# A hybrid decoder step on one core: tables, raw weight pieces and gathers in other buffers and queues

## The chip, the core and the metric

The kernel runs on one core of a Trainium2 chip. The engines have in-order instruction queues of their own and meet through semaphores: TensorE (PE; its weight loads are listed as PEld), VectorE (DVE), ScalarE (ACT), GpSimd (POOL) and SyncE (SP). SP computes nothing; it issues DMAs. DMAs can be issued by ACT and POOL too; the issue is then an instruction in that engine's queue. The metric is the device time of one execution, in microseconds (us). The kernel before takes 752.33 us, the median of three runs (750.71 to 752.95).

## The reference

One layer on a prompt of 1024 tokens and on 8 single new tokens (samples), each with 256 earlier tokens in paged caches:

```python
hn = rms_norm(x, norm_g)                              # D_MODEL = 1024
u, v, z_a, q, kc, vc, ks, vs, kw, vw, g, z_b = split(hn @ w_in)
# gMLP half: layer norm of v, then a causal 128x128 gate per channel group and chunk
vn = layer_norm(v, ln_v_g, ln_v_b)
a  = u * (einsum('gts,bnsgc->bntgc', w_s * tril, vn) + b_s) * silu(z_a)
# attention half: rope on q, ks, kw; 8 query heads, 2 KV heads, three branches
#   compressed blocks, the 16 selected blocks, a window of 512; gated sum
o  = gate0*attn(q, compress(kc, vc)) + gate1*attn(q, selected(ks, vs)) + gate2*attn(q, window(kw, vw))
y  = rms_norm(x + concat([a, o * silu(z_b)]) @ w_out, final_g)
# samples: the same with pages = cache[page_table]; also returned:
# kc, vc, ks, vs of all tokens, the window's kw, vw, and vn of the samples
```

All data are 32-bit floats. The kernel keeps that accuracy by splitting each operand of a product into a high and a low part (`hi` = a rounded copy, `lo` = the rest) and adding three products: hi·hi, lo·hi and hi·lo.

## The kernel before

*x stage* (lines 192 to 242). Eight pieces of x, each with a piece of w_in for the first three feature groups, are loaded into `raw`. ACT writes the high part `xh` (line 205) and a square, DVE the low part `xl`; PE multiplies piece after piece into tiles `pf` (8 pieces, 24 products of 344 columns each). Lines 244 to 270 make 1/rms: PE sums the squares, DVE spreads the result (`rsb`), and PE transposes it (`pr`) into the row `RS`, by which u and z (`uz`) are scaled on DVE and POOL; `ud` stores a copy of `uz`.

*Queries* (lines 318 to 336). Four tiles of query features, t = 0 to 3, 72 products each (8 pieces x 9), evacuated by ACT and rotated (`rotate`, line 298) with the tables `Cq` and `Sq` of lines 289 and 290; the result goes to `qd` in 4 stores per tile.

*v, k columns, v columns* (lines 349 to 553). Three groups of token tiles, i = 0 to 8 (128 tokens each; tile 8 holds the samples): `ptv` (512 columns), `pta` (384) and `ptb` (408). Tiles 0 to 7 take 24 products and tile 8 takes 16. Each of the first eight `ptv` tiles goes on to ACT (`vt`), DVE (statistics, normalising), POOL (times `lng`, plus `lnb`), ACT again (`vh`, line 450), DVE (`vl`, line 451), and then to 12 products of the gate with the split table `wsh`, `wsl` (`pg`, function `gate`). After a gate, `gather` (line 340) issues two page gathers on SP for one of 16 pages (`cg`, `kg`, DRAM to DRAM, 256 rows of 512 bytes each), and `split_wo` (line 417) loads two 128x512 pieces of w_out (`wost`), splits them on ACT and POOL and stores both parts to DRAM. The `pta` tiles are rotated with `ctok` and `stok` (lines 483, 484), split and transposed on PE (`pkt`, line 524); from here `gather` stands behind each store of k rows. After the `ptb` tiles come compression, attention of the samples, attention of the prompt in query blocks, and the output projection, before which both parts of w_out (`woh`, `wol`) are loaded back.

*Weights.* `load_w` (line 134) loads a raw piece (`wst`, 2 or 3 buffers in the pool that also holds the parts), ACT makes its high part (line 143), DVE its low part (line 144), 9 buffers each. `f_weights` makes two pieces for a feature group, `t_weights` eight for a group of token tiles.

*Order.* A scheduler lays out each engine's instructions by priority and by an estimated timeline, from the program as it is traced; buffers come from pools, and a tile in memory that another pool held waits until that pool's tiles are released. `issue_after(ins)` puts what is issued inside it behind `ins` in its engine's queue. All loads and stores shown here are on SP but the page table's.

## Time and profile before

| | |
|---|---|
| median of three runs | 752.33 us |
| profiled execution, its own time | 751.49 us |
| its span | 749.7 us |
| PE busy | 92% of the span |
| DVE, ACT, POOL busy | 69%, 50%, 39% |
| mean granted clock of PE | 0.97 of full speed |
| moved by DMA | 95.48 MB, of which SP's queue 92.26 |

Times in the rows below count from the span's start. A row of the stretches has its start and end, its length, then for PE, PEld, DVE, ACT and POOL the busy us with the count of instructions, the granted clock, the share of the DMA engines and GB/s. A row of waits has who waited, at which tile and line, for whose tile or transfer, then the total in us, how many times, and the longest. A row of a timeline has start and duration in us, engine and line, tile written and read, shape and count, and in brackets the idle time before it with what ended it. A row of groups has a shape, a count, the busy us, the mean in ns of one and the idle time before. A row of a line's instructions has minimum, median and maximum in ns.

### The profile page before, as it was taken

The page shows a single profiled execution, that of the slowest core. Times are in us where ns is not written, and L with a number is a line of the kernel's source. Part 1 is how long each engine was busy: PE and PEld are TensorE (multiplying, and loading weights), DVE is VectorE, ACT ScalarE, POOL GpSimd, SP SyncE. Part 2 cuts the span into 40 slices and gives each one's busy share as a digit, 9 for nine tenths or more (in the row PEclk, how much of TensorE's full clock was granted, in tenths as well). Part 3 has the DMA queues.
Part 4 walks back from the last instruction along what each step waited for, and adds up shares of the span by engine and source line. Part 5 has one row for each costly group of instructions (what it writes and reads, how often), then busy time and mean ns, then how long its engine had stood idle before and what let it go on. Part 6 is the DMA issues. An engine that isn't in the chain of part 4 may idle for free.

```text
span 749.7 us, 12604 instructions
## 1 busy us (share of the span) xinstructions
PE 688.4 (92%) x4186; PEld 631.7 (84%) x4186; DVE 514.1 (69%) x1470; ACT 374.6 (50%) x890; POOL 293.8 (39%) x282
## 2 busy tenths in 40 slices
PE   8989998778866899999999999998999999999994
PEld 6989986658865799987989999887999998888993
DVE  6737882768724317854279997997777899879743
ACT  7523221233114336431158777886666686666631
POOL 0011434745711003343232244468465656555521
PEclk9999999789988999999999999999999999999997
DMA  8056266657543415427253211895121212212011
GB/s 322 21 197 198 70 155 200 184 190 254 188 138 111 152 29 187 156 81 269 75 162 100 63 62 48 317 315 154 41 70 71 72 43 63 67 59 84 15 57 56
DMA packets 71176, 95.48 MB, mean 127 GB/s; under 512 B 5904, under 2 KB 45440, under 8 KB 70312
## 3 DMA queue, kind: packets, MB, share of 16 engines
q1 hardware_dynamic: 70664, 92.26, 38.6%
q0 software_dynamic: 160, 2.15, 0.8%
q8 instruction: 33, 0.54, 0.3%
q14 instruction: 31, 0.25, 0.1%
q10 hardware_dynamic: 288, 0.27, 0.1%
HBM read 67.85 MB, written 33.10 MB: 135 GB/s over the span
## 4 chain that ended last, share of the span: by engine, by line
PE 53%; DVE 14%; DMA 13%; issue 6%; SPq 5%; ACT 4%; POOL 4%; POOLq 0%; ACTq 0%; DVEq 0%
PE pf L45 15%; PE pout L45 10%; PE o L45 7%; PE S L45 6%; PE pt L940 6%; PE ptb L45 3%; DMA wost<-in_w_out 3%; DMA out<-ka 2%; PE pc L45 2%; DMA wst<-in_wF 1%; DMA wst<-in_w_c 1%; DVE Xl L660 1%; DVE Pl L859 1%; PE po L45 1%; DMA qd<-sh 1%
## 5 line engine op out<-in xcount | busy, mean ns | idle before, releaser
L944 DVE TENSOR_TENSOR tl<-pt,th 128x512 fp32r<-128x512 f32 (+1 forms) x160 | 100.9, 643 | 21.1 <-ACT th L943 20.3
L45 PE MATMUL pf<-xh,whi 128*128 128x344 f32 x384 | 109.4, 326 | 2.1 <-ACT xh L205 1.2
L45 PE MATMUL pf<-xl,whi 128*128 128x344 f32 x384 | 109.9, 322 | 0.0
L45 PE MATMUL pf<-xh,wlo 128*128 128x344 f32 x384 | 109.8, 323 | 0.0
L943 ACT CAST th<-pt 128x512 fp32r<-128x512 f32 (+1 forms) x160 | 83.5, 551 | 27.8 <-PE pt L940 25.9
L917 POOL TENSOR_TENSOR Pw<-Pw,r 128x640 f32<-128x640 f32 (+3 forms) x112 | 76.1, 699 | 52.5 <-DVE r L911 28.0
L45 PE MATMUL pout<-woh,mix 128*128 128x512 f32 (+1 forms) x272 | 87.5, 389 | 1.9 <-ACT mix L977 1.8
L917 POOL TENSOR_TENSOR Pl<-Pl,r 128x384 f32<-128x384 f32 (+5 forms) x36 | 49.3, 1369 | 76.7 <-DVE r L911 30.0
L45 PE MATMUL o<-th,v 128*128 128x256 f32 x264 | 74.3, 300 | 1.4 <-ACT th L943 1.3
L45 PEld LDWEIGHTS pf<-xh,whi 128*128 128x128 f32 x384 | 69.7, 189 | 3.7 <-ACT xh L205 2.1
L45 PEld LDWEIGHTS pf<-xl,whi 128*128 128x128 f32 x384 | 70.3, 190 | 1.0 <-issue 0.6
L45 PEld LDWEIGHTS pf<-xh,wlo 128*128 128x128 f32 x384 | 69.9, 189 | 0.3 <-issue 0.2
L45 PE MATMUL o<-tl,v 128*128 128x256 f32 x264 | 69.7, 289 | 0.4 <-DVE tl L944 0.3
L863 ACT ACTIVATE Pl<-Pl,nmx 128x128 f32<-128x128 f32 (+7 forms) x64 | 49.8, 778 | 23.9 <-DVE nmx L859 18.8
L45 PEld LDWEIGHTS pout<-woh,mix 128*128 128x128 f32 x272 | 50.8, 192 | 11.5 <-ACT mix L977 2.0
L903 ACT ACTIVATE Pw<-Pw,nmx 128x640 f32<-128x640 f32 (+4 forms) x64 | 44.6, 696 | 22.2 <-DVE nmx L895 20.9
L45 PE MATMUL S<-kwS,q 128*128 128x384 f32 (+2 forms) x224 | 52.8, 331 | 1.5 <-DVE nmx L901 0.8
L45 PE MATMUL S<-ksS,q 128*128 128x384 f32 (+5 forms) x192 | 51.8, 357 | 2.4 <-DMA q<-qd 1.9
L45 PEld LDWEIGHTS o<-th,v 128*128 128x128 f32 x264 | 49.9, 189 | 4.4 <-ACT th L943 2.1
L45 PEld LDWEIGHTS o<-tl,v 128*128 128x128 f32 x264 | 49.9, 189 | 4.0 <-DVE tl L944 2.8
L45 PE MATMUL pout<-wol,mix 128*128 128x512 f32 (+1 forms) x136 | 52.5, 387 | 0.0
L144 POOL TENSOR_TENSOR wlo<-wst,whi 128x512 fp32r<-128x512 f32 x18 | 24.1, 1342 | 70.0 <-ACT whi L143 51.5
(337 smaller groups left out, 1698.8 us busy)
## 6 DMA issues: line engine op xcount, KB each, us to landing
q<-qd SPq DMA_DIRECT2D x32, 256.0 KB
wst<-in_wF SPq DMA_DIRECT2D x26, 256.0 KB
raw<-in_xw SPq DMA_DIRECT2D x7, 708.0 KB
wost<-in_w_out SPq DMA_DIRECT2D x16, 256.0 KB
wod<-wohi SPq DMA_DIRECT2D x16, 256.0 KB
wod<-wolo SPq DMA_DIRECT2D x16, 256.0 KB
woh<-wod SPq DMA_DIRECT2D x2, 2048.0 KB
wol<-wod SPq DMA_DIRECT2D x2, 2048.0 KB
```

The costliest lines, as they stand in the source:

```text
L45: return pe.matmul(out, lhsT, rhs, start=start, stop=stop, skip_group_check=True)
L144: e.tensor_tensor(lo[:, :n], st[:, :n], f32(hi[:, :n]), op=ALU.subtract)
L660: v.tensor_tensor(dst(Xl), src, f32(hi), op=ALU.subtract)
L859: v.tensor_tensor_reduce(Pl[:, sl], S[:, 0:half], m, -0.125, nmx[:, 0:1] if c else BIG, ALU.add, ALU.min, nmx[:, 0:1])
L863: s.activation(Pl[:, 0:L], Pl[:, 0:L], AF.Exp, bias=nmx[:, 0:1], scale=-1.0, accum_out=sums[:, 1:2])
L903: s.activation(Pw[:, 0:nw], Pw[:, 0:nw], AF.Exp, bias=nmx[:, 1:2], scale=-1.0, accum_out=sums[:, 2:3])
L917: g.tensor_tensor(t_[:, a:b], t_[:, a:b], r[:, j:j + 1].to_broadcast((P, b - a)), op=ALU.mult)
L940: pe.transpose(pt[:, ci * 256 + e * P:ci * 256 + (e + 1) * P], src[e][:, col:col + P], ident)
L943: s.copy(th[:, :n], pt[:, :n])
L944: v.tensor_tensor(tl[:, :n], pt[:, :n], f32(th[:, :n]), op=ALU.subtract)
```

## The change

- The tables `lng`, `lnb`, `wsh` and `wsl` get a pool of their own (`vq`), loaded between pieces 5 and 6 of x and behind the query weights; `ctok` and `stok` are loaded behind the last query rows.
- Raw pieces get a pool of their own: 4 buffers in the query stage, 8 (`wr`) for the `wTa` and `wTb` pieces; they are issued behind a named DMA (`W["behind"]`): the last x piece, `Sq`, the last query store, the second store of k rows.
- Weights of the first two query tiles are loaded in the x stage, those of the last two behind `Sq`; half of the first query tile's products stand ahead of the transposes of `rsb`.
- The 16 page numbers are loaded into ACT's registers, and ACT issues the gathers. A new function `early` is called behind each `vh`, `k2` and `v2` (24 calls): the first 16 issue one `cg` gather and load and split one 128x512 piece of w_out, the last 8 issue two `kg` gathers each. The store of a low part is issued one call later, by ACT.
- High parts of w_out are no longer stored. Before the output projection w_out itself is loaded again, in 8 pieces of 128x1024, and ACT makes `woh` from them.

The diff, cut to its core:

```diff
-            st = wp.tile([P, 512], F32, tag="wst", bufs=W["raw"], name="wst")
-            with tc.issue_after(x_in.ins):
+            st = W["rp"].tile([P, 512], F32, tag="wst", bufs=W["raw"], name="wst")
+            with tc.issue_after(W["behind"].ins):
                 W["dma"] = sy.dma_start(st[:, :n], src)
...
+        vq_ctx = ExitStack()
+        vq = vq_ctx.enter_context(tc.tile_pool(name="vq", bufs=1, side="right", reuse_waits="tile"))
+        lng = vq.tile([P, 512], F32, name="lng")
+        lnb = vq.tile([P, 512], F32, name="lnb")
+        wsh = vq.tile([P, 8, P], F32R, name="wsh")
+        wsl = vq.tile([P, 8, P], F32R, name="wsl")
         wq_ctx = ExitStack()
-        wq = wq_ctx.enter_context(tc.tile_pool(name="wq", bufs=2, side="right", reuse_waits="tile"))
+        wq = wq_ctx.enter_context(tc.tile_pool(name="wq", bufs=4, side="right", reuse_waits="tile"))
...
-        with tc.issue_after(x_in.ins):
-            sy.dma_start(bs, io["b_s"])
-        W["pool"], W["raw"] = wq, 2
-        q_first = f_weights(8)
+        W.update(pool=wq, rp=wq, raw=2, behind=x_in)
+        q_first = [f_weights(8), f_weights(9)]
...
+        sy.dma_start(lng, io["ln_v_g"].partition_broadcast(P))
+        sy.dma_start(lnb, io["ln_v_b"].partition_broadcast(P))
+        sy.dma_start(bs, io["b_s"])
+        ws = sqp.tile([P, wx + TT], F32, tag="xs", bufs=5, name="ws")
+        tril = ws[:, T:T + P]
+        ws = ws[:, 0:T].rearrange("p (a b) -> p a b", a=8)
+        sy.dma_start(ws, io["w_s"])
+        sy.dma_start(tril, io["tril"])
+        g.tensor_tensor(ws, ws, tril.unsqueeze(1).to_broadcast((P, 8, P)), op=ALU.mult)
...
-        W["pool"], W["raw"] = wp_ctx.enter_context(tc.tile_pool(name="wp", bufs=9, reuse_waits="tile")), 3
...
+        qF = f_tiles(1)
+        for k in range(4):
+            q_mm = f_k(q_first[0], qF, k)
...
+              with tc.issue_after(q_mm.ins):
...
+        s.copy(wsh, ws)
+        g.tensor_tensor(wsl, ws, f32(wsh), op=ALU.subtract)
         sy.dma_start(ud, uz[:, 1, :])
         sq_ctx.close()
+        wp = wp_ctx.enter_context(tc.tile_pool(name="wp", bufs=9, reuse_waits="tile"))
+        wr_ctx = ExitStack()
+        wr = wr_ctx.enter_context(tc.tile_pool(name="wr", bufs=4, reuse_waits="tile"))
...
-        sy.dma_start(Sq, io["Sq"])
+        W.update(pool=wp, rp=wr, raw=4, behind=sy.dma_start(Sq, io["Sq"]))
...
-            prow = [sy.value_load(ptb[0:1, j:j + 1], min_val=0, max_val=io["cA"].shape[0] - 1) for j in range(16)]
+        prow = [s.value_load(ptb[0:1, j:j + 1], min_val=0, max_val=io["cA"].shape[0] - 1) for j in range(16)]
...
-            qh = qp.tile([P, T], F32R, tag="qh", bufs=2, name="qh")
+            qh = qp.tile([P, T], F32R, tag="qh", bufs=1, name="qh")
...
-            qF = f_tiles(t)
-            wts = f_weights(8 + t) if t else q_first
-            for k in range(KT):
+            if t:
+                qF = f_tiles(t + 1)
+            wts = f_weights(8 + t) if t > 1 else q_first[t]
+            for k in range(4 if t == 0 else 0, KT):
...
+        wv = [load_w(io["wTv"][k], 512) for k in range(KT)]
+        wr_ctx.close()
+        wr_ctx = ExitStack()
+        wo = wr_ctx.enter_context(tc.tile_pool(name="wo", bufs=2, reuse_waits="tile"))
+        wr = wr_ctx.enter_context(tc.tile_pool(name="wr", bufs=8, reuse_waits="tile"))
+        ctok = wo.tile([P, 9, 16], F32, bufs=1, name="ctok")
+        stok = wo.tile([P, 9, 16], F32, bufs=1, name="stok")
+        with tc.issue_after(W["qd"].ins):
+            sy.dma_start(ctok, io["ctok"])
+            sy.dma_start(stok, io["stok"])
+        W.update(rp=wr, raw=8, behind=W["qd"])
...
+        wo_low = []
+
+        def early(t, behind):
+            half, k = t % 2, t // 2
+            cs_ = slice(half * 512, half * 512 + 512)
             with tc.issue_after(behind.ins):
-                sy.dma_start(cg[:, :, j, :], io["cA"][bass.ds(prow[j], 1)].rearrange("o k p c -> (o k) p c"))
-                sy.dma_start(kg[:, :, j, :], io["cB"][bass.ds(prow[j], 1)].rearrange("o p (k c) -> (o k) p c", k=2))
+                if wo_low:
+                    s.dma_start(*wo_low.pop())
+                if t < 16:
+                    s.dma_start(cg[:, :, t, :], io["cA"][bass.ds(prow[t], 1)].rearrange("o k p c -> (o k) p c"))
+                    st = wo.tile([P, 512], F32, tag="wost", name="wost")
+                    s.dma_start(st, io["w_out"][k, :, cs_])
+                    hi = wo.tile([P, 512], F32R, tag="wohi", bufs=1, name="wohi")
+                    lo = wo.tile([P, 512], F32R, tag="wolo", name="wolo")
+                    s.copy(hi, st)
+                    g.tensor_tensor(lo, st, f32(hi), op=ALU.subtract)
+                    wo_low.append((wol_d[half, :, k, :], f32(lo)))
+                else:
+                    for j in range(2 * t - 32, 2 * t - 30):
+                        s.dma_start(kg[:, :, j, :],
+                                    io["cB"][bass.ds(prow[j], 1)].rearrange("o p (k c) -> (o k) p c", k=2))
...
-            st = sy.dma_start(sd[1:4, :, cols].rearrange("g p c -> p g c"), sp[:, 1:4, :])
-            gather(i, st)
-
-        def split_wo(half, k):
-
-            cs_ = slice(half * 512, half * 512 + 512)
-            st = vp.tile([P, 512], F32, tag="wost", bufs=2, name="wost")
-            hi = vp.tile([P, 512], F32R, tag="wohi", bufs=2, name="wohi")
-            lo = vp.tile([P, 512], F32R, tag="wolo", bufs=2, name="wolo")
-            sy.dma_start(st, io["w_out"][k, :, cs_])
-            s.copy(hi, st)
-            g.tensor_tensor(lo, st, f32(hi), op=ALU.subtract)
-            sy.dma_start(wod[half, 0, :, k, :], f32(hi))
-            sy.dma_start(wod[half, 1, :, k, :], f32(lo))
+            sy.dma_start(sd[1:4, :, cols].rearrange("g p c -> p g c"), sp[:, 1:4, :])
...
+                vh_in = s.copy(vh, vt)
                 v.tensor_tensor(vl, vt, f32(vh), op=ALU.subtract)
                 gate(i, vh, vl)
-                for half in range(2):
-                    split_wo(half, i)
+                early(i, vh_in)
...
-            st = sy.dma_start(o_ks[rows], ka[:, 0:P])
-            gather(8 + i, st)
+            o_in = sy.dma_start(o_ks[rows], ka[:, 0:P])
+            if i == 1:
+                W["behind"] = o_in
...
+            k2_in = s.copy(k2[:, :, 0:64], ka4)
+            early(8 + i, k2_in)
...
+        kq_ctx.close()
         wts = t_weights(io["wTb"], NV)
-        W["pool"], W["raw"] = wf, 2
+        wr_ctx.close()
+        ft_ctx = ExitStack()
+        wf = ft_ctx.enter_context(tc.tile_pool(name="wf", bufs=4, side="right", reuse_waits="tile"))
+        kq_ctx = ExitStack()
+        kq = kq_ctx.enter_context(tc.tile_pool(name="kb", bufs=2, side="right", reuse_waits="tile"))
+        W.update(pool=wf, rp=wf, raw=2)
...
+            v2_in = s.copy(v2[:, i, :, 0:64], vb4)
+            early(16 + i, v2_in)
...
-                for half in range(2):
-                    for hl, w in enumerate((woh, wol)):
-                        sy.dma_start(f32(w[:, :, half * 512:half * 512 + 512]), wod[half, hl])
+                wo_ctx = ExitStack()
+                wop = wo_ctx.enter_context(tc.tile_pool(name="wop", bufs=7, side="right", reuse_waits="tile"))
+                for k in range(KT):
+                    st = wop.tile([P, D], F32, tag="wost", name="wost")
+                    sy.dma_start(st, io["w_out"][k])
+                    s.copy(woh[:, k, :], st)
+                    if k == 6:
+                        for half in range(2):
+                            sy.dma_start(f32(wol[:, :, half * 512:half * 512 + 512]), wol_d[half])
+                wo_ctx.close()
```

SP's queue where the query stage begins; `wF` are query weights, `wTv` those of `ptv`, `wTa` those of `pta`, `ud` the stored copy of `uz`. Before:

```order
L140 DMA wst<-in_wF 128x512 x6
L140 DMA wst<-in_wTv 128x512 x5
L280 DMA ud<-uz 128x1032
L140 DMA wst<-in_wTv 128x512 x3
L289 DMA Cq<-in_Cq 128x1032
L290 DMA Sq<-in_Sq 128x1032
L140 DMA wst<-in_wTa 128x384
L315 DMA qd<-qh 64x8x128 x2
```

and now:

```order
L140 DMA wst<-in_wF 128x512 x4
L243 DMA ws<-in_w_s 128x1024
L244 DMA ws<-in_tril 128x128
L298 DMA ud<-uz 128x1032
L310 DMA Cq<-in_Cq 128x1032
L311 DMA Sq<-in_Sq 128x1032
L140 DMA wst<-in_wF 128x512 x4
L140 DMA wst<-in_wTv 128x512 x5
L335 DMA qd<-qh 64x8x128 x2
```

The first line before holds the weights of three query tiles; now four pieces, two tiles, stand there, and those of the other two are behind `ud`, `Cq` and `Sq`, while the gate's table `ws` (line 243) is ahead of them.

ACT's queue where the first `ptv` tiles are evacuated (`vt`, `vh`; `wohi` is the high part of a w_out piece). Before:

```order
L374 ACTIVATE vt<-ptv,rs 128x512 x2
L424 CAST wohi<-wost 128x512 x2
L393 CAST wsh<-ws 128x1024
L424 CAST wohi<-wost 128x512 x2
L450 CAST vh<-vt 128x512 x2
L374 ACTIVATE vt<-ptv,rs 128x512 x2
L424 CAST wohi<-wost 128x512 x3
L450 CAST vh<-vt 128x512
L424 CAST wohi<-wost 128x512
L450 CAST vh<-vt 128x512
```

and now:

```order
L420 ACTIVATE vt<-ptv,rs 128x512 x2
L143 CAST whi<-wst 128x384
L474 CAST vh<-vt 128x512
L384 ISA
L384 DMA cg<-in_cA 256x128
L386 DMA wost<-in_w_out 128x512
L474 CAST vh<-vt 128x512
L384 ISA
L384 DMA cg<-in_cA 256x128
L386 DMA wost<-in_w_out 128x512
L420 ACTIVATE vt<-ptv,rs 128x512 x2
L389 CAST wohi<-wost 128x512
```

`wsh` is gone from here, `vh` of the first tiles no longer stands behind casts of w_out pieces, and the gather (`cg`), the load of a piece and a step on a register (ISA) stand behind each `vh`.

PE's queue at the seam from the `pta` tiles to the `ptb` tiles (`pkt`: transposes of k rows). Before:

```order
L45 MATMUL pta<-wlo,xsS 128x384
L45 MATMUL ptb<-whi,xh 128x408
L45 MATMUL ptb<-wlo,xh 128x408
L45 MATMUL ptb<-whi,xl 128x408
L45 MATMUL ptb<-whi,xh 128x408 x2
L45 MATMUL ptb<-wlo,xh 128x408 x2
L45 MATMUL ptb<-whi,xl 128x408 x2
L45 MATMUL ptb<-whi,xh 128x408
L45 MATMUL ptb<-wlo,xh 128x408
```

and now:

```order
L45 MATMUL pta<-wlo,xsS 128x384
L45 MATMUL ptb<-whi,xh 128x408
L45 MATMUL ptb<-wlo,xh 128x408
L45 MATMUL ptb<-whi,xl 128x408
L543 MATMUL pkt<-identr,k_2104 128x128 x4
L543 MATMUL pkt<-identr,k_2157 128x128 x4
L45 MATMUL ptb<-whi,xh 128x408
L45 MATMUL ptb<-wlo,xh 128x408
L45 MATMUL ptb<-whi,xl 128x408
L45 MATMUL ptb<-whi,xh 128x408
L45 MATMUL ptb<-wlo,xh 128x408
L45 MATMUL ptb<-whi,xl 128x408
```

The first weight piece of `wTb` is now followed by two groups of transposes before the second tile's products; then the high products of several tiles stand together (x4), where before there were pairs (x2).

## Rows read from the trace of the kernel before

**Rows 1.** Busy time of the engines in three stretches (columns as above).

```profile
10.50:41.10 30.60, 30.60 (x196) 30.52 (x196) 22.05 (x25) 18.85 (x27) 2.00 (x5) 1.00 0.32 117
93.60:282.40 188.80, 154.30 (x756) 136.90 (x755) 101.04 (x256) 52.71 (x117) 64.65 (x50) 0.91 0.52 160
460.00:520.00 60.00, 54.43 (x388) 49.51 (x387) 54.79 (x204) 49.35 (x133) 34.58 (x42) 1.00 0.72 239
```

**Rows 2.** The page's first part, TensorE.

```profile
...
PE 688.4 (92%) x4186; PEld 631.7 (84%) x4186; DVE 514.1 (69%) x1470; ACT 374.6 (50%) x890; POOL 293.8 (39%) x282
...
```

**Rows 3.** Waits of TensorE in the second stretch.

```profile
PE pg L45 <- ACT vh L450: 9.9, 2, 7.4
PE ptb L45 <- ACT whi L143: 8.5, 4, 3.1
PE pkt L524 <- DVE k L521: 8.4, 2, 7.0
PE pg L45 <- DVE vl L451: 3.0, 3, 1.9
PE pta L45 <- DVE wlo L144: 2.1, 2, 1.2
PE pta L45 <- ACT whi L143: 1.6, 2, 1.2
...
```

**Rows 4.** Timeline of TensorE, single places.

```profile
42.74 0.43 PE L45 MATMUL pf<-xh,whi 128*128 128x344 f32 x1
...
54.76 0.44 PE L266 MATMUL pr<-ident,rsb 128*128 128x128 f32 x2 [2.46 <-DVE rsb L262]
...
93.86 0.39 PE L45 MATMUL ptv<-whi,xh 128*128 128x512 f32 x1
...
96.88 0.39 PE L45 MATMUL ptv<-wlo,xh 128*128 128x512 f32 x1
...
134.96 0.80 PE L45 MATMUL pg<-wsh,vh 128*128 128x256 f32 x2 [7.37 <-ACT vh L450]
...
139.03 0.63 PE L45 MATMUL ptv<-wlo,xh 128*128 128x512 f32 x1
...
218.83 0.47 PE L524 MATMUL pkt<-identr,k 128*128 128x128 f32 x2 [7.04 <-DVE k L521]
```

**Rows 5.** Timeline of SyncE, three issues.

```profile
70.46 0.42 SPq L289 DMA_DIRECT2D Cq<-in_Cq  x1
...
115.70 0.44 SPq L387 DMA_DIRECT2D ws<-in_w_s  x1
...
210.26 3.12 SPq L483 DMA_DIRECT2D ctok<-in_ctok  x1
```

**Rows 6.** Waits of ScalarE in the second stretch, the longest.

```profile
ACT wohi L424 <- DMA wost<-in_w_out: 48.4, 12, 11.2
...
```

**Rows 7.** Groups of instructions of TensorE there, one kind.

```profile
...
L45 PE MATMUL ptv<-wlo,xh 128*128 128x512 f32 x64 | 25.8, 404 | 0.0
...
```

**Rows 8.** Groups of VectorE there, low halves of the last weights.

```profile
...
L144 DVE TENSOR_TENSOR wlo<-wst,whi 128x408 fp32r<-128x408 f32 x8 | 6.3, 801 | 10.5 <-ACT whi L143 10.5
...
```

**Rows 9.** Timeline of GpSimd, one pass.

```profile
67.09 2.42 POOL L276 TENSOR_TENSOR uz<-uz,z 128x1032 f32<-128x1032 f32 x1 [25.56 <-DVE z L275]
```

**Rows 10.** All instructions of lines 295 and 343.

```profile
L295 SPq TENSOR_LOAD <-ptb x16: 263/263/478, 16.4 to 25.2; - x16
...
L343 SPq DMA_DIRECT2D cg<-in_cA x16: 557/558/678, 144.9 to 249.6; - x16
```

**Rows 11.** Timeline of ScalarE, two of the x pieces.

```profile
...
11.69 1.16 ACT L205 ACTIVATE xh<-raw,ng 128x1032 fp32r<-128x1032 f32 x1
...
14.11 1.15 ACT L205 ACTIVATE xh<-raw,ng 128x1032 fp32r<-128x1032 f32 x1
...
```

**Rows 12.** The last two stores.

```profile
745.65 0.34 SPq L1053 DMA_DIRECT2D out<-xt  x1
745.86 0.35 ACTq L1054 DMA_DIRECT2D out<-xt  x1
```

More of the change, by code (lines that the diff above doesn't have):

```diff
@@ L76, in trunk @@
         kg = dram.tile([2, P, 16, P], F32, name="kg")
-        wod = dram.tile([2, 2, P, KT, 512], F32, name="wod")
+        wol_d = dram.tile([2, P, KT, 512], F32, name="wol_d")
         qsd = dram.tile([NB, 24], F32, name="qsd")
@@ L156, in f_k @@
             c = (k % 4) * P
-            f_mm(hi[:, c:c + P], lo[:, c:c + P], outs3, k)
+            return f_mm(hi[:, c:c + P], lo[:, c:c + P], outs3, k)
         def f_mm(hi, lo, outs, k, thirds=(0, 1, 2)):
@@ L207, in trunk @@
                                        op0=ALU.mult, op1=ALU.subtract)
-            sq = acc if k == 0 else sqp.tile([P, TT], F32, tag="sq", bufs=5, name="sq")
+            sq = acc if k == 0 else sqp.tile([P, TT], F32, tag="sq", bufs=4, name="sq")
             s.activation(sq, xs, AF.Square)
@@ L272, in trunk @@
         v.tensor_tensor(z0, z0, RS, op=ALU.mult)
-        th0 = sqp.tile([P, TT], F32, tag="sq", bufs=5, name="th0")
+        th0 = sqp.tile([P, TT], F32, tag="sq", bufs=4, name="th0")
         s.activation(th0, z0, AF.Tanh, scale=0.5)
@@ L293, in trunk @@
         swap = list(range(8, 16)) + list(range(0, 8)) + list(range(16, 32))
-        with tc.issue_after(x_in.ins):
-            prow = [sy.value_load(ptb[0:1, j:j + 1], min_val=0, max_val=io["cA"].shape[0] - 1) for j in range(16)]
+        prow = [s.value_load(ptb[0:1, j:j + 1], min_val=0, max_val=io["cA"].shape[0] - 1) for j in range(16)]
         v.tensor_copy(bsx, bs.unsqueeze(2).to_broadcast((P, 8, 64)))
@@ L314, in rotate @@
                 for hl, src in ((0, qh), (1, ql)):
[L315 removed]
+                    W["qd"] = sy.dma_start(qd[:, :, hl, 4 * h + t, :].rearrange("q d c -> d q c"),
                                  f32(src[64 * h:64 * h + 64, :]).rearrange("p (q c) -> p q c", q=8))
@@ L338, in trunk @@
         wq_ctx.close()
-        def gather(j, behind):
-            with tc.issue_after(behind.ins):
-                sy.dma_start(cg[:, :, j, :], io["cA"][bass.ds(prow[j], 1)].rearrange("o k p c -> (o k) p c"))
-                sy.dma_start(kg[:, :, j, :], io["cB"][bass.ds(prow[j], 1)].rearrange("o p (k c) -> (o k) p c", k=2))
+        wv = [load_w(io["wTv"][k], 512) for k in range(KT)]
+        wr_ctx.close()
+        wr_ctx = ExitStack()
+        wo = wr_ctx.enter_context(tc.tile_pool(name="wo", bufs=2, reuse_waits="tile"))
@@ L347, in trunk @@
         vp_ctx = ExitStack()
         vp = vp_ctx.enter_context(tc.tile_pool(name="vp", bufs=1, side="right", reuse_waits="tile"))
-        lng = vp.tile([P, 512], F32, name="lng")
-        lnb = vp.tile([P, 512], F32, name="lnb")
-        sy.dma_start(lng, io["ln_v_g"].partition_broadcast(P))
-        sy.dma_start(lnb, io["ln_v_b"].partition_broadcast(P))
         def t_weights(src, cols):
@@ L379, in t_evac @@
                 v.tensor_scalar(out, out, rs[0:NB, 8:9], None, op0=ALU.mult)
-        ws = vp.tile([P, 8, P], F32, name="ws")
-        tril = vp.tile([P, P], F32, name="tril")
-        wsh = vp.tile([P, 8, P], F32R, name="wsh")
-        wsl = vp.tile([P, 8, P], F32R, name="wsl")
         w00 = vp.tile([NB, 8], F32, name="w00")
         b00 = vp.tile([NB, 8], F32, name="b00")
-        sy.dma_start(ws, io["w_s"])
-        sy.dma_start(tril, io["tril"])
         sy.dma_start(w00, io["w_s"][0:1, :, 0].partition_broadcast(NB))
         sy.dma_start(b00, io["b_s"][0:1, :].partition_broadcast(NB))
-        wts = t_weights(io["wTv"], 512)
-        g.tensor_tensor(ws, ws, tril.unsqueeze(1).to_broadcast((P, 8, P)), op=ALU.mult)
-        s.copy(wsh, ws)
-        g.tensor_tensor(wsl, ws, f32(wsh), op=ALU.subtract)
         def gate(i, vh, vl):
@@ L468, in trunk @@
         vp_ctx.close()
+        vq_ctx.close()
         gm_ctx.close()
@@ L476, in trunk @@
         vc2 = kp.tile([P, 2, P], F32R, name="vc2")
-        ft_ctx = ExitStack()
-        wf = ft_ctx.enter_context(tc.tile_pool(name="wf", bufs=4, side="right", reuse_waits="tile"))
         kq_ctx = ExitStack()
         kq = kq_ctx.enter_context(tc.tile_pool(name="kq", bufs=2, side="right", reuse_waits="tile"))
-        ctok = kq.tile([P, 9, 16], F32, bufs=1, name="ctok")
-        stok = kq.tile([P, 9, 16], F32, bufs=1, name="stok")
-        sy.dma_start(ctok, io["ctok"])
-        sy.dma_start(stok, io["stok"])
         def rope_rows(t, i, n):
```

5 lines of the change are left out of this document (1 added, 4 removed).

## The prediction, made before the changed kernel ran

> **What bounds the kernel now.** I first set the busy time of the engines against the span, stage by stage, then read who TensorE waited for in the stage that fell short, and then the queue that the awaited transfers came from. TensorE (PE) is the bound nearly everywhere, and the question is where it is not. From 10.5 to 41.1 us it is busy all of the time [rows 1]. From 93.6 to 282.4 us, the stage that makes v, the k columns and the v columns (tiles ptv, pta, ptb) and the spatial gate (pg), it is busy 154.30 of 188.80 us, at a mean granted clock of 0.91 [rows 1]. These 34.5 us of idle time are more than half of the 61.3 us that PE idles in the whole span (749.7 of the span less 688.4 busy, [rows 2]).
>
> The waits add up to that: 9.9 us for vh, 8.5 and 2.1 + 1.6 us for split weights, 8.4 us for the k rows, 3.0 us for vl [rows 3]. The longest are single events, 7.37 us at 134.96 and 7.04 us at 218.83 [rows 4]. Behind each stands a transfer that SyncE's (SP's) queue sent late. The table ws of the gate was issued at 115.70 and ctok, the rotation table of the k rows, at 210.26 [rows 5], since both buffers lie in memory that a pool frees only then and since the queue is in order; SP needed 3.12 us to issue ctok, behind a pair of page gathers. ScalarE (ACT) itself waited 48.4 us for pieces of w_out, 12 times, the longest 11.2 us [rows 6], and vh and the weight splits stand behind those casts.
>
> [...]
>
> **The floor of that stage.** Products start 0.232 us apart at the upper level: (96.88 - 93.86) / 13 [rows 4]. The time goes with the columns, so 384, 408 and 256 columns are 0.174, 0.185 and 0.116 us. Tiles 0 to 7 take 24 products each and tile 8 takes 16, 208 per weight group (64 of each of three kinds, [rows 7]); the gate takes 12 for each of 8 tiles. That is 208 x (0.232 + 0.174 + 0.185) + 96 x 0.116 = 122.9 + 11.1 us, and 32 transposes of 128 columns (0.058 each) add 1.9: 136 us. The stage takes 188.8, so it loses 52.8: 34.5 idle and 18.3 at the lower level, 0.53 us of slow running per idle us.
>
> **The change, part by part.**
>
> *Tables early.* lng, lnb and ws get buffers of their own and load during the x stage and the first products; ctok and stok load right behind the last query rows. The 9.9 us for vh goes entirely: what is late next is POOL's two passes over vt, and the order puts tile 0's pg behind five ptv tiles, 120 x 0.232 = 28 us. Of the 8.4 us for k rows I keep 1. The same bytes now load in the x stage, where DMA is at 0.32 [rows 1]; nothing on the path.
>
> *Weights in raw buffers of their own.* Eight raw pieces of wTa and of wTb now wait in SBUF before their turn, so a split waits only for its high and low buffer (still nine). The seam from ptv to pta remains: I keep 2.5 of its 3.7 us. At the seam to ptb PE now works on four tiles per weight piece, 12 x 0.185 = 2.2 us, against 0.80 us for the low half of a split [rows 8]; I keep 1.5 of 8.5. Of the 3.0 for vl I keep 1. So 6 us of idle time stay, with 3.2 of slow running: 136 + 9.2 = 145.2, a gain of **43.6**. The bounds are the floor (52.8) and the case that only the tables' waits go (rivals).
>
> *Queue rows, first part.* The wait of 2.46 us for rsb at 54.76 [rows 4] goes, because no weight split stands in VectorE's (DVE's) queue within that chain any more, and about 1.5 us of slow running with it: gain 4. But the weights of the third query tile now stand in SP's queue behind ud, Cq and Sq, as the rows of SP's order in the section on the change show. Cq waits for POOL's pass over uz (2.42 us at 67.09), and was issued at 70.46 [rows 5, 9]. With the transposes 4 us earlier I expect Cq at about 63, weights landing at 68, and ACT evacuating the second query tile first, at 69; PE has run out at 67.6: the products that follow the x stage start at 42.74 [rows 4], 144 of them come before that point at 30.6 / 192 = 0.159 us each [rows 1], and the transposes of rsb and their neighbours take 1.9. Loss 2.5 and 1.5 of slow running: 4. Together 0, between -4 and +8.
>
> *Page numbers on ACT.* Sixteen loads of 0.263 us [rows 10] go from SP to ACT, three or four behind each of five x pieces: about 1 us on top of ACT's 2.42 per piece (11.69 to 14.11, [rows 11]), under PE's 3.82 (30.6 / 8, [rows 1]). The cover is thin only at the first piece. Bounds 0 and 3 us; I take **+1**, near the cover.
>
> *Gathers and w_out on ACT.* ACT now issues 32 gathers (0.558 us each for one cache and, by that nearest row, as much for the other, [rows 10]) and 32 other transfers of about 0.35 us [rows 12]: 18 + 11 = 29 us on its queue, beside 52.7 us busy of 188.8 [rows 1]. 82 of 145 us leaves it room, but in the ptb stage two gathers per tile stand ahead of the next evacuations, and the 128x128 casts of compress want them all. Bounds 0 and 6; I take **+2**. The 16 stores of high parts vanish; they cost the path nothing once ACT no longer waits for the pieces.
>
> *High parts made late.* Before the output projection ACT casts eight 128x1024 pieces, by the nearest row 1.16 us each (1032 columns, [rows 11]): 9.3 us in a stage (460 to 520) where it is busy 49.35 of 60 and PE 54.43 [rows 1]. The bytes loaded there stay 8 MB. It fits barely; bounds 0 and 9, I take **+2**.
>
> **Sum.** 751.49 us is the profiled execution's own time (its span of 749.7 and 1.8 around it). 751.49 - 43.6 + 0 + 1 + 2 + 2 = 712.9, and as the median shown (752.33) lies 0.84 higher, **714 us**.
>
> [...] ACT's last store was issued at 745.86 while SP's (745.65, 0.34 us) was still going, and took 0.35 us, no more than alone [rows 12]: the two queues did not hold each other up there. [...]
>
> The page counts DMA at 0.52 busy in the slow stage [rows 1], so the engines that carry the transfers have room. [...]
>
> **Rivals.**
> *A. ACT becomes the bound.* Each gather is 256 rows of 512 bytes, and behind a pair of them SP's next issue took 3.12 us [rows 5]. If every one of the 16 w_out casts still waits 2 us (half of 48.4 / 12) and the gathers cost twice their row, ACT has 82 + 32 + 18 = 132 us plus waits for POOL and PE: 14 us of idle time more on PE, 21 with slow running. 714 + 21 = **735**. For it: the order puts vh right before or behind these issues. Against: ACT was 28% busy.
> *B. Only the tables' waits go.* Weights still come late, because wTa stands behind 16 stores of query rows and wTb behind two k tiles. Then 9.9 + 8.4 - 1 = 17.3 goes and 17.2 stays: gain 17.3 x 1.53 = 26.5 for 43.6: **731**. Against: the raw pieces are issued a whole stage ahead.
> *C. Slower.* Each call that issues a page gather and splits a piece of w_out stands in ACT's queue before evacuations that PE waits for. If each of the 16 holds ACT for 4.0 us (48.4 / 12, [rows 6]) and each of 8 pairs of gathers for 2.2 (four times their row), that is 82 us of ACT's queue. With half of it beside PE's work, PE idles 41 us more, 63 with the slow running: 714 + 63 = **777**. It decides from 1.0 us of PE time lost per call (24 calls, 24 us idle, 37 with slow running, and the gain is gone).
> *D. The order changes nothing that matters*, because the late part of the program, with PE at 97% and more, was laid out anew and loses what the stage gains: about 752. Nothing in the rows supports a loss of 38 us there.
>
> **How the numbers follow.** Forecast 0.62 (704 to 724), better than 704 0.04, B 0.14, A 0.13, C 0.05, D 0.02. The range that leaves out 2 in 10 or less goes from the floor with the small costs (about 703) to just beyond A: **703 to 737**. This kernel's runs lie within 0.15% of their median, so 0.3% (2.3 us) tells a change from none. Faster 0.92, same 0.02, slower 0.06.
>
> **What would show it.** After the change PE's idle time between the first ptv and the last ptb is near 6 us, the distance near 145, with no wait over 3 us; the waits for vh and the k rows are gone; ptv starts at 93 to 96 as before (93.86); a wait of 2 to 3 us stands before the third query tile; ACT's waits for w_out fall to under 20 us; in the counterpart of 460 to 520 PE is no more than 2 us worse. The forecast is wrong if ACT's queue shows issue instructions of 2 us in front of evacuations (A), if whi waits for transfers (B), or if PE idles in the ptb stage for ACT (C).

## The result and the profile after

The changed kernel takes 748.1 us (median of 20 runs, 745.39 to 751.66), against 752.79 us for the kernel before in the same sessions: ratio 0.9942, 95% interval [0.9926, 0.9958]. It is faster by 4.4 us where 38 were forecast, and 748.1 lies above the range of 703 to 737. The profiled execution took 745.39 us, its span 743.6.

The first and the last tile of each stage, read from TensorE's tiles in each profile, say where the forecast held. Starts of the first `ptv` product, the last of `ptb`, the first of `pc` (compression), the last of `pf` (features) and the span's end, in us, and the distances between them:

| kernel | ptv | ptb | pc | pf | end | ptv to ptb | ptb to pc | pc to pf | pf to end |
|---|---|---|---|---|---|---|---|---|---|
| before | 93.9 | 282.9 | 295.5 | 470.6 | 749.7 | 189.0 | 12.6 | 175.1 | 279.1 |
| changed | 97.3 | 242.5 | 285.6 | 460.0 | 743.6 | 145.2 | 43.1 | 174.4 | 283.6 |

The stage of `ptv`, `pta` and `ptb` was forecast at 145 us and took 145.2. Of the 43.8 us won there, 30.5 were lost again before the first `pc`, 3.4 ahead of the first `ptv` and 4.5 behind the last feature; 0.7 were won between `pc` and `pf`. Each row is one execution. In the changed kernel and the experiments on it (e4 apart), the first `ptv` starts anywhere from 93.4 to 97.9, so a difference of 2 or 3 us in a single stretch says little by itself.

TensorE's busy time and four stretches of the changed kernel: the x stage, the stage just named (to compare with the second of [rows 1]), the stretch behind it, and the one before the output projection (columns as in [rows 1]).

```profile
PE 683.4 (92%) x4186; PEld 628.1 (84%) x4186; DVE 510.6 (69%) x1470; ACT 383.0 (52%) x898; POOL 294.5 (40%) x282
```

```profile
10.50:41.10 30.60, 29.86 (x189) 29.78 (x190) 23.60 (x28) 21.52 (x30) 3.66 (x4) 1.00 0.47 165
97.30:242.90 145.60, 140.96 (x760) 127.93 (x758) 92.22 (x244) 47.44 (x104) 56.07 (x45) 1.00 0.49 148
243.00:285.60 42.60, 15.24 (x84) 14.66 (x82) 12.32 (x29) 13.27 (x29) 3.44 (x3) 0.69 0.37 115
455.00:517.00 62.00, 54.13 (x356) 45.68 (x355) 51.85 (x190) 52.18 (x127) 35.47 (x40) 0.97 0.67 231
```

The second row has what the forecast named: 4.6 us idle (6 forecast) and a granted clock of 1.00. In the third, TensorE works 15.24 of 42.60 us at a granted clock of 0.69. Its longest three waits from 93 to 300 us; the third is the longest inside the stage. Of [rows 3], 0.8 us for `vl` and 0.9 for split weights are left, and the waits for `vh` and the k rows are gone:

```profile
PE pct L691 <- DVE kccs L586: 21.5, 1, 21.5
PE pc L45 <- ACT Xh L685: 5.9, 1, 5.9
PE ptb L45 <- ACT kvc L528: 1.6, 1, 1.6
```

The wait of 21.5 us ends at 268.04, with transposes (`pct`) of `kvc`, the part of each `ptb` tile that is to be compressed. ACT wrote the last of `kvc` at 266.71. `kccs`, to which the wait is put down, is a small copy at 267.8 that stood in DVE's queue behind DVE's work on the same tile. So TensorE waited for the evacuation of the last tiles. ACT's waits from 195 to 275 us ("issue" is time in which ACT waited for nothing that the profile shows, here its own DMA issues), and its timeline at the end of them:

```profile
ACT vb L568 <- issue: 13.8, 3, 5.4
ACT vb L568 <- DMA wst<-in_wF: 10.6, 2, 6.9
ACT whi L143 <- issue: 6.6, 3, 2.7
ACT gates L580 <- issue: 5.8, 1, 5.8
```

```profile
253.53 0.47 ACT L568 ACTIVATE vb<-ptb,rs 128x256 f32<-128x256 f32 x1 [6.86 <-DMA wst<-in_wF]
253.90 0.36 ACT L569 ACTIVATE kvc<-ptb,rs 128x128 f32<-128x128 f32 x1
254.15 0.40 ACT L576 CAST v<-vb 128x256 fp32r<-128x256 f32 x1
254.18 5.61 ACTq L394 DMA_DIRECT2D kg<-in_cB  x2
259.89 0.47 ACT L568 ACTIVATE vb<-ptb,rs 128x256 f32<-128x256 f32 x1 [5.33 <-issue]
260.26 0.36 ACT L569 ACTIVATE kvc<-ptb,rs 128x128 f32<-128x128 f32 x1
260.51 0.40 ACT L576 CAST v<-vb 128x256 fp32r<-128x256 f32 x1
260.53 5.63 ACTq L394 DMA_DIRECT2D kg<-in_cB  x2
266.34 0.47 ACT L568 ACTIVATE vb<-ptb,rs 128x256 f32<-128x256 f32 x1 [5.43 <-issue]
```

Each of these `ptb` tiles costs ACT three instructions that take 1.0 us together, and then 5.6 us in the issue of two `kg` gathers, with the next tile's evacuation behind them. The first `vb` is put down to a transfer of `wst`, but two issues of 3.21 and 4.13 us stood ahead of it. All 16 issues in one row, with minimum, median and maximum in ns; then those of the same gathers on SP in the kernel before, and the stores of low parts, of which the last two stand among the gathers:

```profile
L394 ACTq DMA_DIRECT2D kg<-in_cB x16: 621/2940/4131, 220.0 to 269.3; - x16
```

```profile
L344 SPq DMA_DIRECT2D kg<-in_cB x16: 666/670/974, 145.8 to 250.3; - x16
```

```profile
L382 ACTq DMA_DIRECT2D wol_d<-wolo x16: 326/333/3487, 128.4 to 231.6; - x16
```

An issue took 2.94 us in the median where it took 0.67 before, issued one at a time with a `cg` gather. A store among them, which has another shape, took up to 3.49 us for 0.33. So an issue's length here comes from what stands ahead of it.

How fast the gathers move is read from the DMA queue of ACT (q10, which moves 12.85 MB in this kernel and 0.27 before; packets, MB, share of the 16 DMA engines). First from 256 to 266 us, when it holds `kg` gathers alone, then from 123.8 to 124.3, when it moves the first `cg` gather:

```profile
q10 hardware_dynamic: 790, 0.40, 13.2%
```

```profile
q10 hardware_dynamic: 203, 0.10, 67.7%
```

A gather of either kind is 256 packets of 512 bytes. The `kg` gathers move 40 GB/s, 3.2 us for one, on 2.1 engines' worth (0.132 x 16); the `cg` gather moves some 200 GB/s on 10.8. Both come to 19 GB/s per busy engine. So a `kg` gather is not slower per busy engine: fewer are busy while it moves, 2.1 in the mean for 10.8. From the first issue to the end of the last ACT needs 53.1 us, 3.3 per gather: it goes at the pace at which they drain.

### The profile page after: what moved, and what is told of

It reads as the page before. It is cut to its first block, busy times and chain, and to the rows that moved or that the text cites. A ratio compares the mean times of both kernels' runs of the same rounds, so it can differ in the third digit from the quotient of the medians.

```text
span 743.6 us, 12579 instructions
## 1 busy us (share of the span) xinstructions
PE 683.4 (92%) x4186; PEld 628.1 (84%) x4186; DVE 510.6 (69%) x1470; ACT 383.0 (52%) x898; POOL 294.5 (40%) x282
## 3 DMA queue, kind: packets, MB, share of 16 engines
q10 hardware_dynamic: 13376, 12.85, 5.4%
## 4 chain that ended last, share of the span: by engine, by line
PE 54%; DVE 12%; DMA 11%; issue 7%; ACTq 6%; ACT 5%; POOL 3%; SPq 1%; POOLq 0%; DVEq 0%
PE pf L45 15%; PE pout L45 11%; PE o L45 8%; PE S L45 7%; PE pt L966 7%; ACTq L394 4%; DMA kg<-in_cB 2%; DMA zd<-z 2%; DMA wost<-in_w_out 1%; PE ptb L45 1%; PE po L45 1%; DVE sp L445 1%; PE pouts L45 1%; POOL vt L469 1%; PE pA L45 1%
## 5 line engine op out<-in xcount | busy, mean ns | idle before, releaser
L45 PEld LDWEIGHTS pf<-xh,whi 128*128 128x128 f32 x384 | 71.2, 195 | 6.7 <-ACT whi L143 3.2
L45 PEld LDWEIGHTS pf<-xl,whi 128*128 128x128 f32 x384 | 71.8, 195 | 1.2 <-issue 1.0
L45 PEld LDWEIGHTS pout<-woh,mix 128*128 128x128 f32 x272 | 49.9, 188 | 10.5 <-ACT mix L1003 2.0
L889 ACT ACTIVATE Pl<-Pl,nmx 128x128 f32<-128x128 f32 (+7 forms) x64 | 49.8, 778 | 15.1 <-DVE nmx L885 12.9
L45 PE MATMUL S<-kwS,q 128*128 128x384 f32 (+2 forms) x224 | 54.9, 336 | 2.9 <-DVE nmx L885 1.9
L45 PE MATMUL S<-ksS,q 128*128 128x384 f32 (+5 forms) x192 | 53.5, 363 | 1.1 <-DVE nmx L885 0.7
L143 ACT CAST whi<-wst 128x512 fp32r<-128x512 f32 (+2 forms) x50 | 28.4, 587 | 41.1 <-DMA wst<-in_wTv 11.9
```

The source lines that it names most:

```text
L45: return pe.matmul(out, lhsT, rhs, start=start, stop=stop, skip_group_check=True)
L143: s.copy(hi[:, :n], st[:, :n])
L889: s.activation(Pl[:, 0:L], Pl[:, 0:L], AF.Exp, bias=nmx[:, 0:1], scale=-1.0, accum_out=sums[:, 1:2])
```

## The experiments

Each changes the changed kernel, unless it says otherwise. Ratios are to the kernel before, run on the same chip; the changed kernel has 0.9942.

### e1: the kg gathers back on SP

```diff
-                        s.dma_start(kg[:, :, j, :], io["cB"][bass.ds(prow[j], 1)]...)   # in early
+            with tc.issue_after(vs_in.ins):          # behind the store of v rows
+                for j in (2 * i, 2 * i + 1):
+                    sy.dma_start(kg[:, :, j, :], io["cB"][bass.ds(prow_sp[j], 1)]...)
```

> The 16 kg gathers go back to SP, two behind each store of v rows in the ptb stage; ACT keeps the 16 cg gathers, the loads of w_out pieces and the stores of low parts. 16 more page numbers are loaded into SP's registers in the x stage. Theory (ACT's queue is held): in the changed kernel the kg issues took 2.94 us in the median, one behind the other on ACT, in front of the evacuations of the ptb tiles, and TensorE waited 21.5 us for them at 268.04. On SP nobody computes behind them: that wait falls under 3 us, TensorE's clock does not fall there, and the stretch from the last ptb product to the first pc product shrinks from 43 to some 13 to 18 us: 748 becomes 718 to 724. Rival (the gathers themselves are the bottleneck, wherever they are issued): SP's stores and the weights of the next features stand behind gathers of 3 us each, TensorE waits for these instead, and the time stays above 738.

Measured 753.09 us, ratio 1.0029 [1.0001, 1.0057], slower than the changed kernel. The rival held. SP's queue and TensorE's two longest waits:

```profile
242.42 2.87 SPq L572 DMA_DIRECT2D out<-vb  x1
245.34 0.42 SPq L574 DMA_DIRECT2D out<-vb  x1
245.96 2.65 SPq L577 DMA_DIRECT2D kg<-in_cB  x2
248.71 3.09 SPq L572 DMA_DIRECT2D out<-vb  x1
```

```profile
PE pc L45 <- ACT Xh L689: 17.3, 1, 17.3
PE pct L695 <- DVE kccs L590: 12.0, 1, 12.0
```

Now the store behind the pair takes the 3 us, as ctok's load did in [rows 5]. ACT waited 15.9 us for `out<-vb`, whose buffers came free late, and 17.9 for `w_c`. A pair came every 7.1 us in the mean here (216.8 to 266.6) and every 6.7 on ACT (220.0 to 267.0): not the issuer, but the pace of the gathers counts.

### e2: the gathers spread over the first 16 calls

```diff
+                    s.dma_start(kg[:, :, t, :], io["cB"][bass.ds(prow[t], 1)]...)   # beside cg, t < 16
```

> All 32 gathers stay on ACT, but each of the first 16 calls of early issues one cg and one kg gather, and the last 8 calls issue none. If it is the density of the issues that costs (16 gathers in 50 us), an issue here takes 0.5 to 0.7 us as the sparse ones did, the wait of 21.5 us is gone and the time is 718 to 726. If each pair costs what two gathers need to move (some 3 us each), ACT is held about 5 us per call in the ptv and pta stages: the evacuations (vt, ka, pkt) come late there, TensorE idles 1 to 2 us per tile for 16 tiles, and the time is 735 to 750. Rival of the bottleneck elsewhere (the ptb evacuations are late for another reason): no change, 748.

Measured 745.26 us, 0.9928 [0.9901, 0.9955]: the time of the second reading, no faster than the changed kernel as far as the intervals tell. The long wait is gone (ptb to pc: 15.2 us), and the stage takes 172.8 us in place of 145.2, with TensorE waiting for ACT and DVE, up to 4.0 us at a time:

```profile
PE pg L45 <- DVE sp L445: 6.4, 5, 2.5
PE pta L45 <- ACT kvc L528: 5.8, 2, 4.0
PE pkt L543 <- DVE k L540: 5.2, 4, 2.1
PE ptb L45 <- ACT kvc L528: 3.9, 1, 3.9
```

The gathers' own issues are short here (0.67 us in the median, the figure of the first reading). The time went to the next issue on ACT, the load of the piece of w_out, 1.64 us in the median where the changed kernel has 0.61, and ACT waited 37.7 us for these pieces:

```profile
L388 ACTq DMA_DIRECT2D wost<-in_w_out x16: 365/1642/3343, 124.6 to 250.1; - x16
```

### e3: rows of 1024 bytes

```diff
-        kg = dram.tile([2, P, 16, P], F32, name="kg")
+        kg = dram.tile([P, 16, 2 * P], F32, name="kg")
-                        s.dma_start(kg[:, :, j, :], io["cB"][...].rearrange("o p (k c) -> (o k) p c", k=2))
+                        s.dma_start(kg[:, j, :], io["cB"][...].rearrange("o p c -> (o p) c"))
...
```

> The kg gathers stay where the change put them, but each moves its 128 KB as 128 rows of 1024 bytes in place of 256 rows of 512 (kg is laid out with k and v side by side, and the two later loads of kg take 512-byte rows in place of contiguous ones). If an issue costs by the row, its median falls from 2.94 to about 1.5 us, the wait of 21.5 us to under 6, and the time is 722 to 730. If it costs by the byte, the median stays near 2.9 us and the time within 4 us of 748.

Measured 718.5 us, 0.9562 [0.9518, 0.9605], below both expectations: the issues fell not to half but to a sixth, no more than [rows 10] has.

```profile
L394 ACTq DMA_DIRECT2D kg<-in_cB x16: 501/502/526, 219.3 to 241.4; - x16
```

Here ptb to pc is 15.1 us. A factor of six for half the rows is not a cost by the row, so two more kernels took the edit apart.

### e5 and e9: the written side, and the order of the loops

```diff
-        kg = dram.tile([2, P, 16, P], F32, name="kg")           # e5
+        kg = dram.tile([16, 2, P, P], F32, name="kg")
...
-                        s.dma_start(kg[:, :, j, :],               # e9
-                                    io["cB"][...].rearrange("o p (k c) -> (o k) p c", k=2))
+                        s.dma_start(kg[:, :, j, :].rearrange("k p c -> p k c"),
+                                    io["cB"][...].rearrange("o p (k c) -> (o p) k c", k=2))
```

> The changed kernel, kg gathers still 256 rows of 512 bytes read from the page in steps of 1024 bytes, but written to one contiguous 128 KB block of DRAM per page (before: 512-byte rows 8 KB apart). Tells the two readings of the 1 KB rows apart, which halved the rows and changed both sides' strides. If it is the count and size of the rows, an issue still has a median near 2.9 us, TensorE still waits some 20 us for the first pct after the ptb tiles, and the time stays at 745 to 751. If it is the stride on the written side, the issues fall to some 0.6 us and the time to 717 to 725.

> The changed kernel with the same 256 rows of 512 bytes per kg gather, from and to the same places; only the order of the copy's loops differs: rows of the page outermost and the two halves (k, v) inside, where the change has the two halves outermost. While only kg gathers move in the changed kernel (255 to 262 us), the DMA engines are busy a tenth (1 in the slices) and 44 GB/s move: two engines of sixteen. Theory (the outermost loop of 2 puts a gather on two engines): the issues fall to 0.5 to 0.7 us, the wait of 21.5 us is gone and the time is 717 to 725, as with rows of 1024 bytes. Rival (the size of the rows): issues of 2.9 us, 745 to 751.

e5: 745.91 us, 0.9938 [0.9915, 0.9962], no change. e9: 716.74 us, 0.955 [0.9514, 0.9586]: the theory, 0.3 us below its range. The issues of e5, then those of e9:

```profile
L394 ACTq DMA_DIRECT2D kg<-in_cB x16: 621/3078/4131, 217.2 to 266.8; - x16
```

```profile
L394 ACTq DMA_DIRECT2D kg<-in_cB x16: 542/542/591, 219.9 to 241.8; - x16
```

e9 moves the same 256 rows of 512 bytes between the same places; only the loop over k and v is inside the loop over rows. So it is neither the size of a row nor the stride on the written side: what counted is the order of the loops, 0.54 us an issue for 2.94. An outermost loop of 2 stands beside 2.1 engines' worth in the changed kernel; in e5, with 3.08 us an issue, the side that is read still has it. How the number of busy engines follows from the loops is not shown. In e9 ACT's queue holds `kg` gathers alone from 238 to 242 us; it then keeps 0.43 of the engines busy, 6.9 of them, beside SP's queue with 0.30:

```profile
q10 hardware_dynamic: 987, 0.47, 42.9%
```

That is 17 GB/s per busy engine, so with the other order of the rows a busy engine moved no more (19 before); more of them were busy, 6.9 in the mean for 2.1. The `cg` gathers are written in the same form as the slow ones, but the rows of their two halves follow each other evenly on both sides, so that they make one loop of 256 (256x128 in ACT's order in the section on the change); they had 10.8 engines' worth above, and their issues took 0.516 us in the median.

### e6: rows of 1024 bytes in the kernel before

> The kernel before with the kg gathers alone changed to 128 rows of 1024 bytes (all on SP, as there). If the gathers' pace held SP's queue there too (32 gathers from 144.9 to 250.3 us, 3.3 us each), half of them now cost little: the store and load pieces behind them are issued earlier, ctok is issued some 8 to 15 us earlier than 210.26, and the time falls from 752 to 730 to 745. Rival: the waits of before come from memory that pools free late, which this does not touch: ws is issued at 115.70 as before, ahead of any gather, and the time stays within 4 us of 752.

The diff is e3's, on SP. Measured 731.97 us, 0.977 [0.9731, 0.9809]. Its stage takes 167.7 us, 21.3 less than before, and ctok is issued at 200.5. What TensorE still waits for there, the longest four ([rows 3] has 9.9, 8.4, 3.0 and 8.5):

```profile
PE pg L45 <- ACT vh L450: 7.5, 2, 6.9
PE pkt L524 <- DVE k L521: 3.2, 1, 3.2
PE pg L45 <- DVE vl L451: 3.1, 3, 1.7
PE ptb L45 <- ACT whi L143: 1.9, 2, 1.4
```

So most of the wait for k rows, and of the wait for the weights of `ptb`, was the queue behind slow gathers; the wait for `vh` was not, since `ws` comes ahead of any gather (113.3).

### e7 and e8: which part of the change won the stage

```diff
-        W.update(rp=wr, raw=8, behind=W["qd"])            # e7: and the pool wr with 2 buffers for 8
+        W.update(rp=wr, raw=2, behind=W["qd"])
+        with tc.issue_after(ad_in.ins):                   # e8: behind the gated rows' store;
+            sy.dma_start(ctok, io["ctok"])                # lng, lnb behind the last query rows
+            sy.dma_start(stok, io["stok"])
```

> On top of the 1 KB rows (718.5 us): the raw pieces of wTa and wTb have 2 buffers in place of 8. Theory (raw pieces in buffers of their own are worth the 14 us of waits for weights and vl that the sum put to them, some 10 idle and 5 of slow running): TensorE waits 2 to 6 us at each of the two seams for whi, and the time is 726 to 734. Rival: with the queue free two buffers keep up, since a split takes 0.8 us and a weight piece is used for 2.2 us or more: within 3 us of 718.5.

> On top of the 1 KB rows: ctok and stok are issued behind the store of the gated rows (ad), and lng and lnb behind the last query rows, as their places were before; ws stays early. Theory (the early tables were worth the 9.9 and 8.4 us of waits): the k rows wait for ctok again, TensorE idles 4 to 8 us before pkt and up to 3 us for the first vh, with slow running 6 to 15 us: 724 to 733. Rival: the late tables came from the queue behind gathers, not from their place, and with it free they land in time: within 3 us of 718.5.

e7: 723.39 us, 0.9661 [0.9616, 0.9706], 4.9 us above e3, between the two expectations; the stage takes 152.8 us for e3's 145.0. Two buffers are one fewer than the kernel before had there. e8: 719.26 us, 0.9581 [0.9534, 0.9628], not told apart from e3: with SP's queue free, ctok issued at 187.6 is early enough, or costs less than the 3 us or so to which these times are known (in its profile the stage takes 148.2).

### e4: query weights ahead of Cq

```diff
+        W.update(pool=wp, rp=wr, raw=4, behind=x_in)
+        q_first += [f_weights(10), f_weights(11)]         # traced ahead of Cq and Sq
```

> The weights of the third and fourth query tile are issued ahead of Cq and Sq on SP; all else as in the changed kernel. Theory: TensorE's waits of 2.51 us at 70.36 and 1.00 at 74.78 come from Cq's wait in that queue; they go, with some 1.5 us of slow running: 748 becomes 743 to 745. Rival: Cq and Sq now arrive later and hold the rotation, so that the query rows, and with them the raw buffers of the fourth tile, are late: TensorE waits 1 to 4 us at the end of the query stage and nothing is gained.

Measured 750.47 us, 0.9982 [0.996, 1.0005]: nothing gained. The two waits went and the first `ptv` started at 88.9 in place of 97.3, but the gate then waited 6.20 us for `vh`, until 123.59:

```profile
123.59 0.80 PE L45 MATMUL pg<-wsh,vh 128*128 128x256 f32 x2 [6.20 <-ACT vh L476]
```

```profile
107.62 1.23 DVE L334 TENSOR_TENSOR sh<-raw,qh 128x1024 fp32r<-128x1024 f32 x1 [0.95 <-ACT qh L329]
...
117.66 0.56 DVE L144 TENSOR_TENSOR wlo<-wst,whi 128x384 fp32r<-128x384 f32 x1 [5.35 <-ACT whi L143]
...
118.33 1.00 DVE L470 TENSOR_SCALAR vt<-vt,mv,rv 128x512 f32<-128x512 f32 x2
```

The rows of DVE show why: it rotates query rows until 108.8, and then the split of a `wTa` piece, which waits 5.35 us for its high part, stands ahead of the normalising of the first `vt`. So `vt` is as late as in the changed kernel, and ptv to ptb took 154.4 us. The rest of its time (pf to end 287.7) was not taken apart.

### e10, e11 and e12: the high parts of w_out

```diff
-                    s.copy(woh[:, k, :], st)                       # e10, on e3
+                    g.tensor_copy(woh[:, k, :], st)
+                    wo_low.append((woh_d[half, :, k, :], f32(hi)))  # e11, on e3; e12, on e9
+                    for w, w_d in ((woh, woh_d), (wol, wol_d)):
+                        sy.dma_start(f32(w[:, :, half * 512:half * 512 + 512]), w_d[half])
...
```

e11 and e12 also give `wohi` a second buffer.

> On top of the 1 KB rows (718.5 us): GpSimd makes the eight 128x1024 high parts of w_out before the output projection, not ACT. From the last feature product to the end the kernel before took 279.4 us and this base 286.4, and ACT was busy 52 of 62 us there with 8 casts of 1.05 us. Theory (those casts on ACT cost the late part some 5 us): 713 to 716. Rival: GpSimd needs some 2.4 us for each and is late with the probabilities instead, 719 to 724; or the late part lost its time by the layout of the order, within 2 us of 718.5.

> On top of the 1 KB rows: the high parts of w_out are stored once more (16 stores by ACT, issued with those of the low parts) and loaded back in two transfers of 2 MB before the output projection, so that no cast stands there. Theory: the late part shrinks from 286.4 us towards 279.4 while 16 more issues of 0.33 us on ACT cost nothing that shows: 711 to 715. Rival: the stores (4 MB more) stand in ACT's queue in front of evacuations as the kg gathers did, and TensorE loses 3 us or more in the pta stage: 718 to 724.

> The two repairs together on the changed kernel: kg gathers with the rows outermost (716.7 us alone) and the high parts of w_out stored and loaded back (worth 4 us on top of the 1 KB rows). If they add, 711 to 714, the fastest of all kernels here; the late part (last feature product to the end) takes 279 to 281 us. If the stores and the gathers meet on ACT and in the DMA engines, 715 to 718.

e10: 716.1 us, 0.9538 [0.95, 0.9577], between its theory (713 to 716) and no gain at all, which its interval does not tell apart. e11: 714.21 us, 0.9527 [0.9489, 0.9565], in the range of its theory. e12: 715.69 us, 0.9542 [0.9513, 0.957], in the range in which the repairs do not add, though its late stretch is as short as they would make it. From the last feature to the end e3 takes 286.1 us, e10 282.7, e11 279.2 (before: 279.1), e12 280.7. In all nine kernels here in which ACT casts late, the stretch takes 283.1 to 288.2 us; in the four that load stored high parts (before, e6, e11, e12) it takes 279.1 to 281.5. That gives the cost of casting late: 4.6 to 6.9 us of this stretch (e12 against e9, e11 against e3). The totals do not tell e9 to e12 apart, as their intervals overlap. Part of the gain may go to the 16 further issues on ACT: the stage takes 147.7 us in e11 for 145.0 in e3, and 149.4 in e12 for 147.6 in e9; single executions do not settle it.

## Why the prediction was wrong

- **The floor and the stage: right in size, to the tenth by luck.** 136 us of products, 6 idle and 3.2 of slow running were forecast; 145.2 came out. But the stretch has 4.6 us idle and, at a granted clock of 1.00, next to no slow running, so its 141.0 us busy are 5 more than the floor. The 0.53 us of slow running per idle us, by which the 3.2 us here and the rivals' sums were set, is an average over one stage; no run shows it as the price of a gap. What the trace of the kernel before shows is a granted clock of 1.00 at the first products of `ptv` (0.39 us each, the upper level), of 0.50 from 135 to 140 us, behind the gap of 7.37 us (0.63 us each, the lower), and of 1.00 behind the gaps of 1.78 us before 247.03 and 1.74 before 258.69 (columns as in [rows 1]):

```profile
93.60:97.00 3.40, 3.40 (x17) 2.82 (x16) 2.55 (x4) 1.54 (x4) 1.08 (x1) 1.00 0.88 244
135.00:140.00 5.00, 5.00 (x18) 4.30 (x19) 4.96 (x12) 2.25 (x4) 2.38 (x2) 0.50 0.81 238
247.10:250.00 2.90, 2.90 (x16) 2.90 (x17) 2.90 (x9) 1.99 (x6) 0.00 (x0) 1.00 0.40 122
258.70:261.50 2.80, 2.80 (x15) 2.78 (x16) 0.80 (x2) 1.37 (x5) 0.00 (x0) 1.00 0.00 1
```

- **Where the stage's gain came from: half wrong.** I gave 17.3 us of idle time to the tables and some 10 to the weights. e8 shows that the place of ctok, lng and lnb is worth nothing that the times show once the queue is free, and e7 gives the raw buffers 7.8 us of the stage. In the kernel before, e6 wins 21.3 us, about half of the 43.8, by the shape of the gathers alone, out of the tables' waits and the weights' alike. The rest was not split further (`ws` early, w_out's pieces and gathers off SP).
- **Page gathers on ACT: the step that failed.** "ACT now issues 32 gathers (0.558 us each for one cache and, by that nearest row, as much for the other, [rows 10])", and +2 for it all, with bounds of 0 and 6. That is the price of an issue made one at a time; the row of the other cache (0.67) would have said no more. Sixteen `kg` gathers that drain at 3.2 us each, issued two per tile, hold ACT from 220.0 to 273.1, and the evacuations that TensorE needs stand among them; the seam cost 30.5 us. e9, which changes nothing but the order of loops in these gathers, brings the seam to 14.3. The rows had the sign: ctok's load took 3.12 us behind a pair [rows 5], and I read that as SP's matter.
- **Rivals A and C named it in part.** A said that ACT would be the bound, with gathers at twice their row, C that TensorE would idle for ACT behind the `ptb` stage's calls. The sign given for A, issues of 2 us in front of evacuations, is what the trace has, and the time lies above A's 735. Both spread a price over all calls: the first 16 cost the stage nothing that shows (`cg` 0.516 us), the last 8 all of it. SP's issues took no longer beside ACT's long ones, as the short stores of [rows 12] had not beside each other: SP issued at 260.77, 267.23, 267.74 and 269.35 in 0.34 to 0.42 us, inside ACT's issues of 5.63 us from 260.53 and 6.14 us from 266.99.

```profile
260.77 0.42 SPq L574 DMA_DIRECT2D out<-vb  x1
...
267.23 0.42 SPq L574 DMA_DIRECT2D out<-vb  x1
267.74 0.38 SPq L579 DMA_DIRECT2D out<-kvc  x1
269.35 0.34 SPq L668 DMA_DIRECT2D wst<-in_w_c  x1
```

- **Queue rows, first part: right in its mechanism.** The 2.46 us for rsb went, Cq was issued at 63.4 and TensorE waited 2.51 us at 70.36 for the third tile's weights. e4 shows that removing this is worth nothing, since DVE is late next.
- **High parts made late: too small.** +2 was forecast within 0 to 9; the late stretch is 4.5 us longer than before in the changed kernel, and 6.9 longer in e3 than in e11. From 455 to 517 us TensorE idles 7.9 us, for 5.6 in the counterpart before.
- **Page numbers on ACT: not separated.** ptv started 3.4 us later than before, where +1 and 0 were forecast for all that comes ahead of it; in the stretch from 10.5 to 41.1 us TensorE idles 0.7 us where it idled none. No experiment moves these loads alone, and the start scatters by as much.
- **Noise.** The three runs of the kernel before lie up to 0.22% from their median, not 0.15%; nothing hung on it.

With the two wrong terms as measured, 712.9 + (30.5 - 2) + (4.5 - 2) = 743.9, against 745.39 of the profiled execution; the 1.5 us left are 2.4 more ahead of the first `ptv`, 0.2 more gain in the stage and 0.7 won from `pc` to `pf`.
